# Attention queries: stored in DRAM as high and low parts and read into three slots in turn, instead of split after each load

## The chip, the cores and the metric

The kernel runs on one core of one Trainium2 chip. The metric is device time in microseconds of one execution; the median of several runs counts. Engines are named as in the profile: PE is TensorE (matmuls; PEld its weight loads), DVE is VectorE, ACT is ScalarE, POOL is GpSimd, and SP is SyncE, whose queue issues all the DMAs spoken of here. Each engine takes its instructions strictly in the order of the program and waits on semaphores.

## What is computed

The reference is a two-layer decoder trunk on one sequence of 2048 positions and 1024 features. Layer 0 runs a gated linear recurrence (RG-LRU) and a multi-head latent attention side by side, gates both with SiLU and projects them back; layer 1 is a Mamba-2 SSD mixer; each ends in a residual and a LayerNorm. The change touches only the attention:

```
q = rmsnorm(c_q) @ w_uq                # 8 heads, 64 plain + 32 rotary values each
q_rope = rope(q[..., 64:], cos, sin)
s = (q_nope . k_nope + q_rope . k_rope) * 96 ** -0.5      # causal
p = softmax(s);  y = p @ v
```

The kernel keeps float32 precision out of a matmul type that rounds its operands (float32r): a value x is split into a high part, x rounded to float32r, and a low part, x minus the high part. A product is the sum of three matmuls, high by high, high by low and low by high.

## The kernel before

The program is one instruction list per engine, written out by a Python class. Work is put off with `later(lag, fn)`: the function is called, and so its instructions are written, after `lag` more calls of `tick()`, which stand between the units of matmuls. This order is fixed when the program is built; nothing is reordered at run time.

The stages around the change:

- **Keys and values** (`qkv_begin`, L595): 16 units of keys, each split into one of ten slots of the tile `ring` (128 partitions x 1024, high part in columns 0 to 511, low part in 512 to 1023), then stored to the DRAM tile `d_k`, 512 KB each.
- **Queries** (`phase_qkv`, L641): 32 units, one for each group of a head and a chunk of 512 positions, in the order of `GROUPS` (L35): head pairs 0 to 3, within a pair the chunks 3, 2, 1, 0 (3, 0, 1, 2 for the last pair), within a chunk the two heads. A unit has six matmuls into one of eight PSUM buffers. Its `post` (L660), written one unit later, makes the 128 x 512 float32 tile `qf` (four buffers): DVE multiplies the rotary half by the table (L663), ACT scales and copies the plain half (L664), and SP stores `qf` to `d_q`, 256 KB (L665). In the first eight units the loads of keys into ring slots 0 to 7 (L694, L687) and eight units of values (L602, posts on ACT and DVE) are interleaved.
- **Attention** (`phase_attn`, L708): for each group n, the scores of four rows of 128 queries against all chunks of keys up to the diagonal (three matmuls each, L741 to L743, plus the mask, L745), DVE's maximum of each bank (L746) and the row's minimum of the negated maxima (L750), ACT's exponential with its sum (L762). The transposes of the probabilities (L786), their split (L792 and L129) and the product with the values (L815) of the group before are put between. Group n reads its query from ring slot 8 + n % 2 (L729). Groups of chunk 0 are short (four score banks), those of chunk 3 long (16).

How a query comes back: `load_q(n)` (L698) has SP load `d_q` into a staging tile `st`, one of two buffers shared with the loads of weights. `split_q(n)` (L703) has POOL make the high part (L705) and subtract for the low part (L129, the line of the helper `lo`). In group n the split of group n + 1 is written after the second score bank (L853) and the load of group n + 2 after the third (L855). Group 0's load and split and group 1's load are written inside the query stage (L679 to L682).

SP's queue in the attention also holds, for each group, the load of the next pair's keys (L687, which waits for PE), the store of the softmax sums' reciprocals to `d_li` (L775), the loads of these and of the gate (L811, L812), and the store of the finished output (L834).

Of the kernel before, what the change touches and what calls it, by code (L numbers as in the profile page):

```python
# [7 lines left out]
F32 = mybir.dt.float32  # L8
F32R = mybir.dt.float32r
I32 = mybir.dt.int32  # L10
AF = mybir.ActivationFunctionType
ALU = mybir.AluOpType
AX = mybir.AxisListType

P = 128
# [3 lines left out]
NCH = SEQ // CH  # L19
# [38 lines left out]
class K:  # L58
# [96 lines left out]
    def run(self):  # L155
        nc, tc, A = self.nc, self.tc, self.A
        with ExitStack() as ctx:
            dp = ctx.enter_context(tc.tile_pool(name="dram", bufs=1, space=bass.MemoryType.DRAM))
            core = ctx.enter_context(tc.tile_pool(name="core", bufs=1))
            ctx.enter_context(tc.manual_schedule())  # L160
            self.W = core.tile([P, 10, 2048], F32R, name="W")
            self.core = core
            self.stp = ctx.enter_context(tc.tile_pool(name="stp", bufs=2))
            self.ring = core.tile([P, 10, 1024], F32R, name="ring")
            self.cst = core.tile([P, NCST], F32, name="cst")
            self.im = core.tile([P, 2, 128], F32R, name="im")
            self.half = core.tile([P, 2], F32, name="half")
            nc.vector.memset(self.half[:, 0:1], -0.5)
            nc.vector.memset(self.half[:, 1:2], 0.5)
            self.ident = self.cst[:, C_ID:C_ID + 128]  # L170
            D = self.D = {}
            D["y0"] = dp.tile([NT, P, KB, P], F32, name="d_y0")
            D["sg"] = dp.tile([4, P, SEQ], F32, name="d_sg")
            D["kr"] = dp.tile([NCH, P, 2, 512], F32R, name="d_kr")
            D["q"] = dp.tile([8, NCH, P, 512], F32, name="d_q")
            D["k"] = dp.tile([4, NCH, P, 2, 512], F32R, name="d_k")
            D["x1"] = dp.tile([SEQ, DM], F32, name="d_x1")
            D["x1T"] = dp.tile([NCH, P, KB, 2, 512], F32R, name="d_x1T")
            D["li"] = dp.tile([len(GROUPS), 512], F32, name="d_li")
            D["cs"] = dp.tile([NT, 32, P], F32, name="d_cs")  # L180
            D["tab"] = dp.tile([NCH, 4, P, 4, 5, 8], F32, name="d_tab")
            D["y1"] = dp.tile([NT, P, 16, P], F32, name="d_y1")
            self.pp = ctx.enter_context(tc.tile_pool(name="ps", bufs=8, space=bass.MemoryType.PSUM))
            self.layer0()
            with ExitStack() as c2:
                self.l1c = c2.enter_context(tc.tile_pool(name="l1c", bufs=1))
                self.xst = self.l1c.tile([P, 2, 512], F32, name="xst")
                self.o0 = ExitStack()
                self.phase_out0(self.o0.enter_context(tc.tile_pool(name="o0", bufs=2)))
                with ExitStack() as c3:  # L190
                    self.phase_ssd(c3)
                    self.flush_of("phase_ssd")
            self.phase_out1()
            self.dump()
# [444 lines left out]
        self.vunit = vunit  # L639

    def phase_qkv(self):  # L641
        nc, p = self.nc, self.a3
        cT, D = self.cT, self.D
        T = {}

        def factors(c):

            pt = self.psum()
            for t in range(4):
                nc.tensor.transpose(pt[0:64, t * 128:t * 128 + 128], self.rope[:, 4 * c + t], self.ident)  # L650
            t = T[c] = p.tile([P, 512], F32, tag=f"T{c}", name=f"T{c}", bufs=1)
            for e in range(2):
                nc.scalar.activation(out=t[64 * e:64 * e + 64], in_=pt[0:64], func=AF.Copy, scale=SCALE)

        def qunit(h, c):
            ps = self.psum()
            w = lambda s, kb: self.W[:, 8 + kb, s * 1024 + h * 128:s * 1024 + h * 128 + 128]
            self.mm3(ps, [((w(0, kb), w(1, kb)), (cT[c][:, 0, kb], cT[c][:, 1, kb])) for kb in range(2)])

            def post():  # L660
                qf = p.tile([P, 512], F32, tag="qf", name="qf", bufs=4)
                r, o = (slice(64, 128), slice(0, 64))[::1 - 2 * (h % 2)]
                nc.vector.tensor_tensor(out=qf[r], in0=ps[r], in1=T[c][r], op=ALU.mult)  # L663
                nc.scalar.activation(out=qf[o], in_=ps[o], func=AF.Copy, scale=SCALE)  # L664
                nc.sync.dma_start(out=D["q"][h, c], in_=qf)  # L665
            self.later(2, post)

        for c in (3, 0, 2, 1):
            factors(c)
        self.qst = {}  # L670
        for n, (pr, c, e) in enumerate(GROUPS):
            if n < 8:
                self.attn_kv(n)
            qunit(2 * pr + e, c)
            self.tick()
            if n < 16 - 4 * VB:
                self.vunit(4 * VB + n)
                self.tick()
            if n in (12, 20):  # L679
                self.load_q(n // 20)  # L680
            if n == 16:
                self.split_q(0)  # L682


    def load_k(self, pr, kc, e):
# [4 lines left out]
    def attn_kv(self, i):  # L690
# [4 lines left out]
                               in_=self.D["kr"][kc, r].bitcast(F32).rearrange("p s n -> p (s n)"))  # L695
        self.load_k(0, kc, e)

    def load_q(self, n):  # L698
        pr, c, e = GROUPS[n]
        self.qst[n] = self.stp.tile([P, 512], F32, tag="st", name="st")  # L700
        self.nc.sync.dma_start(out=self.qst[n], in_=self.D["q"][2 * pr + e, c])

    def split_q(self, n):  # L703
        nc, st, t = self.nc, self.qst.pop(n), self.ring[:, 8 + n % 2, :]
        nc.gpsimd.tensor_scalar(out=t[:, 0:512], in0=st, scalar1=1.0, scalar2=0.0, op0=ALU.mult, op1=ALU.add)  # L705
        self.lo(nc.gpsimd, t[:, 512:1024], st, t[:, 0:512])

    def phase_attn(self):  # L708
        nc, A, p, v = self.nc, self.A, self.at, self.nc.vector
        vv = self.W[:, 0:8, :].rearrange("p h (k n) -> p h k n", n=128)  # L710
        ring, D = self.ring, self.D
        N = len(GROUPS)

        im = self.im
        ptx = p.tile([P, 2, 1024], F32R, name="ptx")

        g, li, y = (p.tile([P, 512], F32, name=k) for k in ("g", "li", "y"))
        half = lambda e: slice(64 * e, 64 * e + 64)
# [7 lines left out]
        def scores(n, i):  # L726

            pr, c, e = GROUPS[n]
            q = ring[:, 8 + n % 2, :]  # L729
            qh, ql = q[:, i * 128:i * 128 + 128], q[:, 512 + i * 128:512 + i * 128 + 128]  # L730
            m, banks = mx[(4 * n + i) % 6], {}
            nm = m[:, 4:5] if c else m[:, 0:1]
# [45 lines left out]
        def trans():  # L778

            n, kb = ready.pop(0)  # L780
            pr, c, e = GROUPS[n]
            i0 = max(0, kb - 4 * c)
            ps = self.psum()
            for i in range(i0, 4):
                o = 512 * c * i + 64 * i * (i + 1) + kb * 128
                nc.tensor.transpose(ps[:, i * 128:i * 128 + 128], prob[n][:, o:o + 128], self.ident)  # L786
            self.cnt += 1
            k = self.cnt % 6
            hl = self.W[:, 8 + k // 2, k % 2 * 1024:k % 2 * 1024 + 1024] if k < 4 else ptx[:, k - 4]
            hl = hl.rearrange("p (s n) -> p s n", s=2)  # L790
            w = slice(128 * i0, 512)
            self.later(TL, lambda: nc.scalar.copy(hl[:, 0, w], ps[:, w]))  # L792
            self.later(TL + 1, lambda: self.lo(v, hl[:, 1, w], ps[:, w], hl[:, 0, w]))
            flow.append((n, kb, hl, w))
            if kb == 4 * c + 3:
                prob[n] = None
            if len(flow) > LAG:
                pv()
            self.tick()
# [47 lines left out]
        for n in range(N):  # L847
            pr, c, e = GROUPS[n]
            su = [b for i in range(4) for b in scores(n, i)]
            for i, s in enumerate(su):  # L850
                s()
                self.tick()
                if i == 1 and n + 1 < N:  # L853
                    self.split_q(n + 1)
                if i == 2 and n + 2 < N:  # L855
                    self.load_q(n + 2)
                for _ in range(-(-len(ready) // (len(su) - i + SLACK))):
                    trans()
            if pr < 3:
                self.load_k(pr + 1, c, e)  # L860
            k = n - (N - 9)
            if 0 <= k < 6:
                self.load_at(0, k, A["wo0"][k], 7, (nc.gpsimd, nc.gpsimd))
# [739 lines left out]
```

## Time and profile before

| what | us |
|---|---|
| median of 3 runs | 2680.57 (2680.3 to 2682.99) |
| the profiled execution's own time | 2678.24 |
| its span, first to last instruction | 2676.4 |
| query stage | about 410 to 462 |
| attention | about 462 to 930 |
| POOL's 32 splits, each | 0.62 (L705) + 1.29 (L129) |
| mean granted TensorE clock | 0.994 |

The profile is of one execution. Busy time is summed by engine; a group of instructions has its line, engine, operation and tiles. Idle time just before an instruction is put down to whatever released it: `[2.58 <-POOL ring L705]` means that the engine stood still for 2.58 us until a POOL instruction of line 705, which writes the tile ring, was done. In the list of waits the numbers are the total, how often, and the longest. A row of a table of stretches has the stretch, its length, the busy time of PE, PEld, DVE, ACT and POOL with the number of instructions, the granted TensorE clock as a share of full speed, the busy share of the DMA engines and their GB/s. In rows ordered by time the first two numbers are start and length. "To landing" is the time from the issue of a DMA to its completion.

### The profile page before, as it was taken

To read this page: it belongs to the slowest core of one execution; us is meant where nothing else is said; L and a number is where in the kernel's file an instruction comes from. 1 tells how busy PE (TensorE), PEld (TensorE's weight loads), DVE (VectorE), ACT (ScalarE), POOL (GpSimd) and SP (SyncE) were. 2 spreads that over 40 slices of the span, in tenths; PEclk is the share of its full clock that TensorE was granted. 3 is DMA by queue.
4 is the path that set the end of the run, shared out by engine and by line. 5 is a ranking of instruction groups with operands and counts; after the bars stand their busy time and mean duration, and the time that the engine had idled before them with its cause. 6 is when DMAs were issued, how large, how long until landed. Compare 5 with 4: busy or idle time off the path is not lost.

```text
span 2676.4 us, 40050 instructions
## 1 busy us (share of the span) xinstructions
PE 2610.1 (98%) x14504; PEld 2153.2 (80%) x14504; DVE 1749.6 (65%) x3245; ACT 1531.1 (57%) x3178; POOL 944.2 (35%) x880
## 2 busy tenths in 40 slices
PE   8999999999999999999999999999999999899998
PEld 6888987878787878788888888888888888778886
DVE  7767236878787867875667666666677567745532
ACT  5665335877777732234677766766677667642100
POOL 4446211132324544550334223432343222434421
PEclk9999999999999999999999999999999999999999
DMA  4223328241424456682334333433343333455421
GB/s 140 59 87 118 113 90 284 44 72 43 72 53 85 74 174 196 214 266 95 112 132 159 112 112 108 164 114 112 128 157 123 107 105 118 154 184 210 173 95 40
DMA packets 173111, 334.23 MB, mean 125 GB/s; under 512 B 31985, under 2 KB 90225, under 8 KB 169457
## 3 DMA queue, kind: packets, MB, share of 16 engines
q1 hardware_dynamic: 172912, 331.66, 39.8%
q8 instruction: 115, 1.88, 0.3%
q14 instruction: 84, 0.68, 0.1%
HBM read 245.82 MB, written 85.79 MB: 124 GB/s over the span
## 4 chain that ended last, share of the span: by engine, by line
PE 73%; DVE 10%; ACT 6%; DMA 5%; issue 3%; POOL 1%; SPq 0%; ACTq 0%; POOLq 0%; DVEq 0%
PE ps L1159 9%; PE ps L1161 9%; PE ps L1160 9%; PE ps L137 5%; PE ps L139 4%; PE ps L138 4%; PE ps L786 4%; PE ps L815 4%; PE ps L1409 3%; PE ps L1408 3%; PE ps L1407 3%; PE ps L1262 2%; PE ps L921 2%; PE ps L923 2%; PE ps L922 2%
## 5 line engine op out<-in xcount | busy, mean ns | idle before, releaser
L1159 PE MATMUL ps<-ring,W 128*128 128x512 f32 x768 | 304.6, 397 | 0.0
L1161 PE MATMUL ps<-ring,W 128*128 128x512 f32 x768 | 300.1, 391 | 0.0
L1160 PE MATMUL ps<-ring,W 128*128 128x512 f32 x768 | 299.2, 390 | 0.0
L746 DVE TENSOR_REDUCE mx<-ps 128x1 f32<-128x512 f32 (+3 forms) x320 | 193.5, 608 | 73.9 <-PE ps L743 48.7
L1281 POOL TENSOR_TENSOR y<-y,xs 128x512 f32<-128x512 f32 x60 | 78.8, 1313 | 427.6 <-DVE y L1280 427.6
L762 ACT ACTIVATE pr<-ps,mx 128x512 f32<-128x512 f32 (+3 forms) x320 | 198.5, 629 | 15.8 <-DVE mx L750 11.0
L1159 PE MATMUL ps<-W,ring 128*128 128x512 f32 x512 | 201.3, 393 | 0.0
L1161 PE MATMUL ps<-W,ring 128*128 128x512 f32 x512 | 200.3, 391 | 0.0
L1160 PE MATMUL ps<-W,ring 128*128 128x512 f32 x512 | 199.9, 390 | 0.0
L786 PE MATMUL ps<-cst,pr 128*128 128x128 f32 x1088 | 176.6, 277 | 8.1 <-ACT pr L762 5.9
L1212 ACT ACTIVATE e<-e,tab 128x128 f32<-128x128 f32 x512 | 156.4, 390 | 41.8 <-DMA e<-d_cs 41.8
L1161 PEld LDWEIGHTS ps<-ring,W 128*128 128x128 f32 x768 | 144.1, 188 | 31.2
L1159 PEld LDWEIGHTS ps<-ring,W 128*128 128x128 f32 x768 | 144.3, 188 | 29.7 <-ACT yo L1313 0.9
L1160 PEld LDWEIGHTS ps<-ring,W 128*128 128x128 f32 x768 | 144.4, 188 | 28.9
L129 DVE TENSOR_TENSOR W<-ps,W 128x512 fp32r<-128x512 f32 (+3 forms) x261 | 145.0, 561 | 30.8 <-ACT W L613 18.8
L786 PEld LDWEIGHTS ps<-cst,pr 128*128 128x128 f32 x1088 | 130.6, 142 | 42.0 <-ACT pr L762 11.0
L1127 ACT ACT_TABLE_LOAD x58 | 74.4, 1283 | 149.0 <-DVE xT L1125 79.2
L1392 ACT CAST ring<-ring 128x1024 fp32r<-128x1024 f32 x50 | 50.3, 1045 | 188.7 <-PE ps L1408 99.3
L129 POOL TENSOR_TENSOR ring<-ring 128x1024 fp32r<-128x1024 f32 (+1 forms) x41 | 84.5, 2062 | 189.0 <-ACT ring L1392 160.1
L792 ACT CAST W<-ps 128x512 fp32r<-128x512 f32 (+2 forms) x213 | 110.8, 526 | 67.0 <-PE ps L786 63.0
L129 POOL TENSOR_TENSOR W<-st,W 128x512 fp32r<-128x512 f32 (+2 forms) x70 | 111.4, 1598 | 105.0 <-ACT W L112 90.2
L1125 DVE SCALAR_TENSOR_TENSOR xT<-ps,vec,xT 128x509 f32<-128x509 f32 (+2 forms) x192 | 143.2, 746 | 5.0
(347 smaller groups left out, 7509.7 us busy)
## 6 DMA issues: line engine op xcount, KB each, us to landing
ring<-d_x1T SPq DMA_DIRECT2D x128, 512.0 KB, 7.4
e<-d_cs SPq DMA_DIRECT2D x64, 512.0 KB, 4.4
ring<-d_y SPq DMA_DIRECT2D x25, 1024.0 KB, 4.8
st<-in_w_dram SPq DMA_DIRECT2D x40, 512.0 KB, 5.7
d_x1T<-xt SPq DMA_DIRECT2D x32, 512.0 KB, 4.0
d_y<-yo SPq DMA_DIRECT2D x64, 256.0 KB, 4.9
st<-in_wo_dram SPq DMA_DIRECT2D x24, 512.0 KB, 3.8
xs<-in_xT_dram SPq DMA_DIRECT2D x23, 512.0 KB, 3.9
```

The costliest lines, as they stand in the source:

```text
L129: eng.tensor_tensor(out=out, in0=src, in1=hi.bitcast(F32), op=ALU.subtract)
L137: self.nc.tensor.matmul(ps, ah, bh, start=(i == 0), stop=False)
L138: self.nc.tensor.matmul(ps, ah, bl, start=False, stop=False)
L746: v.tensor_reduce(out=m[:, kc:kc + 1], in_=ps[:, 0:nw], axis=AX.X, op=ALU.max, negate=True)
L762: nc.scalar.activation(out=prob[n][:, o:o + nw], in_=ps[:, 0:nw], func=AF.Exp, bias=nm, accum_out=acc)
L786: nc.tensor.transpose(ps[:, i * 128:i * 128 + 128], prob[n][:, o:o + 128], self.ident)
L792: self.later(TL, lambda: nc.scalar.copy(hl[:, 0, w], ps[:, w]))
L1125: v.scalar_tensor_tensor(out=dst, in0=src, scalar=w(k), in1=dst, op0=ALU.mult, op1=ALU.add)
L1159: nc.tensor.matmul(ps, ah, bh, start=(k == 0), stop=False)
L1160: nc.tensor.matmul(ps, ah, bl, start=False, stop=False)
L1161: nc.tensor.matmul(ps, al, bh, start=False, stop=(k == KB - 1))
L1212: nc.scalar.activation(out=e[:, hd], in_=e[:, hd], func=AF.Relu, scale=-1.0, bias=cs[:, hd:hd + 1])
```

## The change

The queries are split where they are made. `d_q` holds both parts (512 KB for each group). In the query stage the store moves out of `post` into a function `split(qf)`, written one tick after it: the high part is copied into a ring slot (ACT for even n, DVE for odd n; L670 in the new program), POOL subtracts the low part, and SP stores the slot to `d_q` (L672). The slot is 8 + n % 2 for n below 26, and 9 from there on.

In the attention there is no split. `load_q(n)` (L707) reads both parts straight into a slot: ring slot 8, the new tile `q2`, or ring slot 9, in turn (n % 3). Group 0's load is written in the query stage after unit 30, those of groups 1 and 2 at the start of the attention, and that of group n + 2 after the first score bank of group n.

```diff
-            D["q"] = dp.tile([8, NCH, P, 512], F32, name="d_q")
+            D["q"] = dp.tile([8, NCH, P, 2, 512], F32R, name="d_q")
...
-        def qunit(h, c):
+        def qunit(n, h, c):
...
                 nc.scalar.activation(out=qf[o], in_=ps[o], func=AF.Copy, scale=SCALE)
-                nc.sync.dma_start(out=D["q"][h, c], in_=qf)
+                self.later(1, lambda: split(qf))
+
+            def split(qf):
+
+                hl = self.ring[:, 8 + n % 2 if n < 26 else 9].rearrange("p (s n) -> p s n", s=2)
+                (v.tensor_copy if n % 2 else nc.scalar.copy)(hl[:, 0], qf)
+                self.lo(nc.gpsimd, hl[:, 1], qf, hl[:, 0])
+                nc.sync.dma_start(out=D["q"][h, c].bitcast(F32), in_=hl.bitcast(F32))
             self.later(2, post)
...
-            if n in (12, 20):
-                self.load_q(n // 20)
-            if n == 16:
-                self.split_q(0)
+            if n == 30:
+                self.load_q(0)
...
+    def qslot(self, n):
+        return (self.ring[:, 8], self.q2, self.ring[:, 9])[n % 3] if n else self.ring[:, 8]
+
     def load_q(self, n):
         pr, c, e = GROUPS[n]
-        self.qst[n] = self.stp.tile([P, 512], F32, tag="st", name="st")
-        self.nc.sync.dma_start(out=self.qst[n], in_=self.D["q"][2 * pr + e, c])
-
-    def split_q(self, n):
-        nc, st, t = self.nc, self.qst.pop(n), self.ring[:, 8 + n % 2, :]
-        nc.gpsimd.tensor_scalar(out=t[:, 0:512], in0=st, scalar1=1.0, scalar2=0.0, op0=ALU.mult, op1=ALU.add)
-        self.lo(nc.gpsimd, t[:, 512:1024], st, t[:, 0:512])
+        self.nc.sync.dma_start(out=self.qslot(n).bitcast(F32), in_=self.D["q"][2 * pr + e, c].bitcast(F32).rearrange("p s n -> p (s n)"))
...
+        self.q2 = p.tile([P, 1024], F32R, name="q2")
+        for n in (1, 2):
+            self.load_q(n)
...
-            q = ring[:, 8 + n % 2, :]
+            q = self.qslot(n)
...
-                if i == 1 and n + 1 < N:
-                    self.split_q(n + 1)
-                if i == 2 and n + 2 < N:
+                if i == 0 and 0 < n < N - 2:
                     self.load_q(n + 2)
```

More of the change, by code (lines that the diff above doesn't have):

```diff
@@ L641, in phase_qkv @@
     def phase_qkv(self):
-        nc, p = self.nc, self.a3
+        nc, p, v = self.nc, self.a3, self.nc.vector
         cT, D = self.cT, self.D
@@ L669, in phase_qkv @@
             factors(c)
-        self.qst = {}
         for n, (pr, c, e) in enumerate(GROUPS):
@@ L673, in phase_qkv @@
                 self.attn_kv(n)
-            qunit(2 * pr + e, c)
+            qunit(n, 2 * pr + e, c)
             self.tick()
```

## The prediction

> **What bounds the kernel now.** I read the page's first part, then the table of stretches around the edited code, then the waits of TensorE in the attention, then the engines' rows in order of time where the two stages meet.
>
> ```profile
> span 2676.4 us, 40050 instructions
> PE 2610.1 (98%) x14504; PEld 2153.2 (80%) x14504; DVE 1749.6 (65%) x3245; ACT 1531.1 (57%) x3178; POOL 944.2 (35%) x880
> 410.00:465.00 55.00, 54.62 (x235) 42.82 (x235) 32.20 (x55) 29.05 (x57) 3.82 (x4) 1.00 0.91 305
> ```
>
> TensorE is busy 98% of the span, so a change pays only where TensorE waits, and costs wherever it makes it wait. The third row is the stage that makes the queries (columns: stretch, its length, then PE, PEld, DVE, ACT, POOL busy, granted clock, DMA share, GB/s): TensorE is full, POOL nearly unused, DMA 0.91 busy. The attention follows, to about 930 us; TensorE's waits in it, longest in total first:
>
> ```profile
> PE ps L741 <- POOL ring L705: 6.5, 3, 2.6
> PE ps L786 <- ACT pr L762: 4.7, 8, 0.8
> PE ps L743 <- POOL ring L129: 3.0, 4, 0.9
> ```
>
> Waits for POOL's split are 6.5 + 3.0 = 9.5 us, in three places and a trace of a fourth. Where they stand the granted clock drops as well (column after POOL):
>
> ```profile
> 560.00:580.00 20.00, 16.51 (x107) 14.51 (x107) 13.45 (x33) 12.77 (x37) 7.52 (x7) 0.96 0.58 85
> 580.00:600.00 20.00, 19.11 (x95) 14.96 (x94) 15.98 (x37) 14.38 (x42) 7.66 (x7) 0.95 0.43 83
> 700.00:720.00 20.00, 17.88 (x85) 14.40 (x86) 14.97 (x36) 12.19 (x36) 9.32 (x9) 0.91 0.37 84
> 820.00:840.00 20.00, 16.19 (x76) 13.08 (x75) 11.81 (x26) 8.79 (x25) 8.54 (x8) 0.83 0.54 93
> ```
>
> **What goes from the attention.** TensorE's busy time at the missing clock is 16.51 x 0.04 + 19.11 x 0.05 + 17.88 x 0.09 + 16.19 x 0.17 = 6.0 us; these stretches are slow because the wait let the clock fall. With the wait gone, both go: 9.5 + 6.0 = 15.5 us. The lower bound is 9.5 (the clock falls for another reason). Of POOL's 32 splits the rest lay beside other work and is worth nothing.
>
> What is late next? The first such place is group 8, and the load was late because of its place in SP's queue:
>
> ```profile
> 558.26 0.45 SPq L687 DMA_DIRECT2D ring<-d_k  x1
> 564.95 0.59 SPq L701 DMA_DIRECT2D st<-d_q  x1
> 576.25 0.62 POOL L705 TENSOR_SCALAR ring<-st 128x512 fp32r<-128x512 f32 x1 [9.60 <-DMA st<-d_q]
> 576.93 0.33 PE L741 MATMUL ps<-ring 128*128 128x128 f32 x1 [2.58 <-POOL ring L705]
> d_li<-ls SPq DMA_DIRECT2D x28, 2.0 KB, 12.0
> ```
>
> SP's queue from the end of group 5, before (d_li is the 2 KB store of the softmax sums, st the staging tile):
>
> ```order
> L687 DMA ring_66<-d_k_76 64x1024 [waits PE_49]
> L811 DMA li_3751<-d_li_79 64x512 [waits DMAHW7_49,DMAHW2_49]
> L812 DMA g_3750<-d_sg_73 64x512 [waits DMAHW3_49]
> L775 DMA d_li_79<-ls1_3760 128x4x1 [waits DMAHW4_49,DVE_49]
> L834 DMA d_y0_72<-y_3752 64x4x128 [waits DMAHW5_49,Pool_49]
> L701 DMA st_4932<-d_q_75 128x512 [waits DMAHW6_49]
> ```
>
> and after, the same stretch:
>
> ```order
> L691 DMA ring_66<-d_k_76 64x1024 [waits DMAHW1_49,PE_49]
> L707 DMA ring_66<-d_q_75 128x1024 [waits PE_49]
> L815 DMA li_3813<-d_li_79 64x512 [waits DMAHW3_49,DMAHW0_49]
> L816 DMA g_3812<-d_sg_73 64x512 [waits DMAHW4_49]
> L779 DMA d_li_79<-ls1_3822 128x4x1 [waits DMAHW5_49,DVE_49]
> L838 DMA d_y0_72<-y_3814 64x4x128 [waits DMAHW6_49,Pool_49]
> ```
>
> The load of group 8 moves ahead of the slow d_li store: about 559 instead of 564.95 us on this clock. Even with the 11 us that it takes now (564.95 to 576.2) it lands near 570, and TensorE asks at 576.93 - 2.58 = 574.35. So I count the gain whole. The loads double to 512 KB, at a DMA share of 0.37 to 0.58: nothing.
>
> **What comes into the query stage.** Each of 32 units now copies its high part into a slot (ACT for even units, DVE for odd), subtracts on POOL, and stores 512 KB; the slot is free for the next unit only when that store has landed. Slots 8 and 9 alternate up to unit 25; units 26 to 31 all use slot 9. The links, from the same forms elsewhere in the trace (the copies, the subtraction, its hand-over from ACT, the stores):
>
> ```profile
> L221 ACT CAST ring<-xs x29: 606/618/645, 36.0 to 332.9; 128x512 fp32r<-128x512 f32 x29
> L221 DVE CAST ring<-xs x3: 413/415/416, 67.4 to 165.1; 128x512 fp32r<-128x512 f32 x3
> L129 POOL TENSOR_TENSOR ring<-st,ring x32: 1261/1286/1297, 447.4 to 916.2; 128x512 fp32r<-128x512 f32 x32
> 399.24 1.06 ACT L586 CAST W<-st 128x1024 fp32r<-128x1024 f32 x1
> 400.38 2.40 POOL L129 TENSOR_TENSOR W<-st,W 128x1024 fp32r<-128x1024 f32 x1 [12.00 <-ACT W L586]
> L626 SPq DMA_DIRECT2D d_k<-ring x16: 319/326/1352, 387.4 to 414.4; - x16
> DMA to landing us min/median/max: 2.6/3.7/5.3
> d_q<-qf SPq DMA_DIRECT2D x32, 256.0 KB, 2.1
> ```
>
> d_k's store is the nearest row for the new one: 512 KB from a ring slot to a DRAM tile of the same form. Its median of 3.7 us has several stores in flight; here one or two are, so I take the 2.6. A hand-over is 0.08 us (399.24 + 1.06 to 400.38), three per cycle 0.2. One cycle of a slot: 0.62 + 1.29 + 2.6 + 0.2 = 4.7 us with the copy on ACT, 4.5 on DVE. Bounds: 2.1 us landing (the 256 KB row) and 3.7. Two slots give a unit every 2.35 us, one slot every 4.6. TensorE makes a unit in 6 matmuls, and starts one 0.7 us after three:
>
> ```profile
> 437.77 0.47 PE L137 MATMUL ps<-cT,W 128*128 128x512 f32 x1
> 438.54 0.40 PE L137 MATMUL ps<-cT,W 128*128 128x512 f32 x1
> 439.24 0.39 PE L137 MATMUL ps<-cT,W 128*128 128x512 f32 x1
> 411.53 0.69 DVE L663 TENSOR_TENSOR qf<-ps,T 64x512 f32<-64x512 f32 x1
> 437.65 2.19 DVE L663 TENSOR_TENSOR qf<-ps,T 64x512 f32<-64x512 f32 x3
> 461.89 0.68 DVE L663 TENSOR_TENSOR qf<-ps,T 64x512 f32<-64x512 f32 x1 [0.63 <-ACT qf L664]
> 462.50 0.27 DVE L746 TENSOR_REDUCE mx<-ps 128x1 f32<-128x128 f32 x1
> 462.97 2.05 DVE L746 TENSOR_REDUCE mx<-ps 128x1 f32<-128x512 f32 x3 [0.19 <-PE ps L743]
> 465.05 0.16 DVE L750 TENSOR_REDUCE mx<-mx 128x1 f32<-128x4 f32 x1
> 465.32 1.28 ACT L762 ACT_TABLE_LOAD   x1 [2.11 <-DMA d_q<-qf]
> ```
>
> So 1.4 us a unit now (three starts from 437.77 to 439.24): the slots become slower than TensorE. The wait stands on ACT and DVE, and both run in order. DVE at the end of the stage, before (the products of the last two units, then the first row's maxima):
>
> ```order
> L663 TENSOR_TENSOR qf_3736<-ps_3718,T2_3295 64x512 [waits DMAHW0_49,PE_49,Activation_49]
> L663 TENSOR_TENSOR qf_3740<-ps_3729,T2_3295 64x512 [waits DMAHW1_49,PE_49,Activation_49]
> L746 TENSOR_REDUCE mx0_3753<-ps_3766 128x1 [waits PE_49]
> L746 TENSOR_REDUCE mx0_3753<-ps_3772 128x1 [waits PE_49]
> L746 TENSOR_REDUCE mx0_3753<-ps_3779 128x1 [waits PE_49]
> ```
>
> and after, where L670 is the copy into the slot and DMAHW the landing of the store ahead:
>
> ```order
> L670 CAST ring_66<-qf_3748 128x512 [waits DMAHW5_49,DMAHW6_49,DVE_49,Pool_49]
> L663 TENSOR_TENSOR qf_3774<-ps_3754,T1_3303 64x512 [waits PE_49]
> L663 TENSOR_TENSOR qf_3788<-ps_3767,T2_3295 64x512 [waits PE_49]
> L670 CAST ring_66<-qf_3774 128x512 [waits DMAHW0_49,DMAHW7_49,DVE_49,Pool_49]
> L663 TENSOR_TENSOR qf_3794<-ps_3781,T2_3295 64x512 [waits PE_49]
> L670 CAST ring_66<-qf_3794 128x512 [waits DMAHW2_49,DMAHW3_49,DVE_49,Pool_49]
> L750 TENSOR_REDUCE mx0_3815<-ps_3828 128x1 [waits PE_49]
> ```
>
> The attention's maxima, and behind them ACT's exponentials, are queued behind the copy of unit 31. When does that run? Units 0 to 8 are paced by DVE and ACT already (411.53 to 437.65); one more copy per unit, (0.62 + 0.42) / 2 = 0.5 us, puts unit 8's product near 441.7, and its copy, behind two activations, at 443. From 8 to 24 eight cycles: 443 + 8 x 4.7 = 480.6. Unit 25's subtraction follows unit 24's on POOL and ends at 480.6 + 0.7 + 2 x 1.29 = 483.9; its store lands 486.5; copies 26 to 31 are five cycles apart from first to last, 3 x 4.7 + 2 x 4.5 = 23.1, so copy 31 starts at 486.6 + 23.1 = 509.7 and ends at 510.1. Four maxima and the minimum (0.27 + 2.05 + 0.16, some 0.2 between) end at 512.8, where ACT loads its table; now that is at 465.32. Delay: 47.5 us. Fourteen landings lie in the chain: 2.1 us would make it 40.5, 3.7 us 63; unit 8's start is good to about 3 us. POOL's part (32 x 1.29 us) is in the cycle; that two-input work with DVE at its side could slow it is inside these bounds.
>
> **Sum.** 2678.24 (the profiled execution: span 2676.4 and 1.84 around it) + 47.5 - 15.5 = 2710.2. The median of the runs shown, 2680.57, is 2.3 higher, so I forecast 2712 us, 1.2% slower. What a measurement here can tell from no change is about 0.2%, 5 us.
>
> **The rivals.**
>
> *Faster: the slots never bind.* Store and subtraction hide behind TensorE, and only the gain is left: 2680.6 - 15.5 = 2665. It decides if a slot's cycle is under two units of TensorE, 2.8 us. For it: POOL is idle there, and the old store had four buffers and hardly stalled. Against: 1.29 + 2.1 alone are 3.4. Chance 0.07; that gain and delay cancel, 0.02.
>
> *Stores land at the median.* 3.7 us, since DMA is 0.91 busy in this stage: 47.5 becomes 63, 2728. Against: the waiting thins the stores out. The Trainium skill (DMA: Bandwidth & Descriptors, Bandwidth) lists 0.95 us for 64 KB and 6.15 us for 1 MB, which I interpolate to an estimate of 3.4 us for 512 KB; by that the sum would be about 2723. Those were loads on another issue path; the row here says 2.6 at its quickest. Chance 0.18.
>
> *The loads stay late.* The change doesn't do what it is said to do in the attention: d_li stores still sit before the loads, TensorE waits as now: 2712 + 15.5 = 2727. Against: the queue above. Chance 0.12.
>
> *TensorE works ahead.* While the copies wait it fills all eight PSUM buffers with scores, 8 x 0.7 = 5.6 us done in the shade: 2707. Against: now too it meets full buffers at once in group 0, paced by ACT:
>
> ```profile
> 467.12 0.44 PE L741 MATMUL ps<-ring 128*128 128x384 f32 x1 [0.29 <-ACT pr L762]
> ```
>
> Chance 0.06. My forecast: 0.55.
>
> **Range.** Its low end is the quick store, 2712 - 7 = 2705, less 5.6 for working ahead and 2 for unit 8: 2697. Its high end is the slow store with the loads nearly all late, 2728 + 10 = 2738. Slower takes all but the first rival and its neighbour: 0.91; same 0.02; faster 0.07.
>
> **What would show it.** The ACT table load of the attention's first exponential near 513 us; copies L670 whose idle time ends on the landing of d_q's store, about 2 to 3 us each; POOL's subtractions 2.35 us apart in the stage's middle and 4.6 us at its end; TensorE with a hole of tens of us before 513; no wait of L741 or L743 for POOL or for the load of q, and a clock of 1.00 in the four stretches, moved by the delay. If the stage ends before 480 us, or TensorE waits for ring at the starts of groups 8, 16 and 24, a step is wrong.

## The result, and the profile after

| | us |
|---|---|
| changed kernel, median of 4 runs | 2718.5 (2715.94 to 2720.53) |
| kernel before, on the same chip, median of 4 | 2681.78 (2680.3 to 2683.98) |
| ratio | 1.0136, 95% interval 1.0118 to 1.0153 |
| the profiled execution after, its own time and span | 2720.29, 2718.5 |

The change costs 36.7 us. The forecast was 2712 us, 31 us (1.2%) over the median shown then.

The first rows of the page, and the rows of the lines that are new (of a copy: durations in ns as least/median/most, first and last start in us; below them what ended their idle time, with total and count; then how long d_q's stores, L672, take to land):

```profile
span 2718.5 us, 40043 instructions
PE 2614.4 (96%) x14504; PEld 2153.2 (79%) x14504; DVE 1757.5 (65%) x3261; ACT 1541.3 (57%) x3194; POOL 922.6 (34%) x848
L670 ACT CAST ring<-qf x16: 617/620/622, 418.1 to 512.9; 128x512 fp32r<-128x512 f32 x16
L670 DVE CAST ring<-qf x16: 418/427/1032, 421.5 to 517.6; 128x512 fp32r<-128x512 f32 x16
  DMA d_q<-ring: 67.4, 26
DMA to landing us min/median/max: 2.6/2.6/4.7
```

TensorE does the same work (2614.4 us busy, 2610.1 before) in a span 42.1 us longer. ACT and DVE stand still for 67.4 us before the copies into the slots, 26 times, until a store of d_q has landed (one more wait, of 2.9 us, is put down to ACT). The slots bind. The landing row rests on few stores: the trace tells the landing of three of the 32.

ACT in order of time, even units only (start, duration, idle before and its releaser): unit 8, the three after it, unit 24, the last units 26, 28 and 30, and the table load of the first exponential:

```profile
447.71 0.62 ACT L670 CAST ring<-qf 128x512 fp32r<-128x512 f32 x1
452.43 0.62 ACT L670 CAST ring<-qf 128x512 fp32r<-128x512 f32 x1 [0.94 <-DMA d_q<-ring]
457.13 0.62 ACT L670 CAST ring<-qf 128x512 fp32r<-128x512 f32 x1 [0.97 <-DMA d_q<-ring]
461.83 0.62 ACT L670 CAST ring<-qf 128x512 fp32r<-128x512 f32 x1 [1.04 <-DMA d_q<-ring]
...
487.09 0.62 ACT L670 CAST ring<-qf 128x512 fp32r<-128x512 f32 x1 [0.20 <-DMA d_q<-ring]
494.17 0.62 ACT L670 CAST ring<-qf 128x512 fp32r<-128x512 f32 x1 [2.75 <-DMA d_q<-ring]
503.36 0.62 ACT L670 CAST ring<-qf 128x512 fp32r<-128x512 f32 x1 [2.73 <-DMA d_q<-ring]
512.86 0.62 ACT L670 CAST ring<-qf 128x512 fp32r<-128x512 f32 x1 [2.72 <-DMA d_q<-ring]
520.30 1.28 ACT L766 ACT_TABLE_LOAD   x1 [6.82 <-DVE mx L754]
```

The cycle of a slot is read from row to row: 4.7 us three times running, and 9.2 to 9.5 us for two units where one slot is left. The table load comes 55.0 us later than before (465.32).

Unit 31's copy on DVE, SP's load of the first group and its time to landing, TensorE's first score, the semaphore waits of that line on TensorE's sequencer (in ns, the longest is 27284), the waits of the queries' matmuls (410 to 530 us), and the granted clock where TensorE waits (column after POOL):

```profile
517.59 0.43 DVE L670 CAST ring<-qf 128x512 fp32r<-128x512 f32 x1 [8.08 <-DMA d_q<-ring]
505.77 0.37 SPq L707 DMA_DIRECT2D ring<-d_q  x1
DMA to landing us min/median/max: 3.9/3.9/3.9
509.87 0.45 PE L745 MATMUL ps<-ring 128*128 128x128 f32 x1 [25.79 <-DVE qf L663]
L745 PEldq EVENT_SEMAPHORE  x165: 51/51/27284, 482.4 to 976.2; - x165
PE ps L137 <- ACT qf L664: 15.8, 17, 2.8
480.00:500.00 20.00, 1.67 (x6) 1.04 (x6) 6.51 (x11) 5.40 (x9) 8.22 (x7) 0.71 0.42 172
500.00:520.00 20.00, 7.96 (x26) 6.38 (x26) 4.22 (x9) 3.01 (x5) 5.71 (x5) 0.61 0.34 131
```

Up to 482 us TensorE waits 17 times, 15.8 us in all, for ACT to empty a buffer. It has made unit 31 by 484.08. Then it stands still for 25.79 us, and this wait is of another kind: ACT has emptied the buffer that the first score needs (unit 24's) by 483.62, and what is missing is the query of group 0. Its load is written after unit 30, so it stands in SP's queue behind unit 30's late store, is issued at 505.77 and lands at 509.67. The row of the first score names DVE's product of unit 31 (done at 509.51) instead, but the sequencer's wait from 482.4, 27.28 us long, ends with the landing. This wait doesn't set the table load: the eight banks that TensorE can fill are done by 517.83, before DVE has ended unit 31's copy (518.02) and can begin the maxima.

In the attention the waits for the split are gone. TensorE's longest waits there, 540 to 985 us, and its clock in three stretches that stand about where the slow ones of before stood, moved by the delay:

```profile
PE ps L790 <- ACT pr L766: 5.0, 8, 1.1
PE ps L819 <- ACT pr L766: 2.2, 3, 0.7
PE ps L790 <- DVE W L129: 1.1, 3, 0.4
620.00:640.00 20.00, 19.23 (x123) 16.45 (x122) 15.95 (x38) 14.31 (x40) 2.55 (x2) 1.00 0.70 102
740.00:760.00 20.00, 19.27 (x123) 16.81 (x122) 16.57 (x37) 13.56 (x38) 2.55 (x2) 1.00 0.75 73
860.00:880.00 20.00, 19.28 (x122) 16.61 (x120) 16.65 (x38) 13.78 (x39) 2.56 (x2) 1.00 0.68 100
```

No wait for POOL or for a load of q is left among them, and the clock is full. The attention ends where the first matmul of the next stage's line begins (L921 before, L923 now: first and last start behind the durations):

```profile
L921 PE MATMUL ps<-W,ring x256: 388/389/498, 957.3 to 1167.9; 128*128 128x512 f32 x128
```

```profile
L923 PE MATMUL ps<-W,ring x256: 388/389/498, 998.0 to 1208.5; 128*128 128x512 f32 x128
```

So the attention runs to 957.3 us in the trace of before, not to the 930 of the table further up. With these three marks (unit 0's product on DVE, the table load, this first matmul) the time splits in two: before 411.53, 465.32, 957.3; now 413.30, 520.30, 998.0. The table load is 55.0 us later, of which 1.8 is there before unit 0 is done; from the table load to the end of the attention it takes 477.7 us instead of 492.0, 14.3 less. The rest of the program keeps the 40.7 us and adds 1.4.

### The profile page after: what moved, and what is told of

It reads as the page before. It is cut to its first block, busy times and chain, and to the rows that moved or that the text cites. A ratio compares the mean times of both kernels' runs of the same rounds, so it can differ in the third digit from the quotient of the medians.

```text
span 2718.5 us, 40043 instructions
## 1 busy us (share of the span) xinstructions
PE 2614.4 (96%) x14504; PEld 2153.2 (79%) x14504; DVE 1757.5 (65%) x3261; ACT 1541.3 (57%) x3194; POOL 922.6 (34%) x848
## 4 chain that ended last, share of the span: by engine, by line
PE 74%; DVE 10%; ACT 6%; DMA 5%; issue 3%; POOL 2%; SPq 0%; ACTq 0%; DVEq 0%; POOLq 0%
PE ps L1161 9%; PE ps L1163 9%; PE ps L1162 9%; PE ps L137 5%; PE ps L139 4%; PE ps L138 4%; PE ps L819 4%; PE ps L790 4%; PE ps L1410 4%; PE ps L1409 4%; PE ps L1411 4%; DMA d_q<-ring 2%; PE ps L1264 2%; PE ps L923 2%; PE ps L925 2%
## 5 line engine op out<-in xcount | busy, mean ns | idle before, releaser
L1129 ACT ACT_TABLE_LOAD x58 | 74.4, 1283 | 148.7 <-DVE xT L1127 79.2
```

## The experiments

Theory: in the query stage the slots' cycle (copy, subtraction, landing) sets the pace, and the delay passes whole to the end; in the attention the gain comes from the load's place ahead of d_li's store in SP's queue. Rivals: the stage is bound by POOL or by the bytes, whatever the slots; and the gain comes from taking the split off POOL.

The runs came on four chips, each beside before: 2681.51 us (median of 13) for the first four, 2696.58 (14) for the next three, 2697.52 (15) for the four after, 2697.02 (17) for the last. Kernels are compared with before of their own row, and with each other on one chip only.

| kernel | median us | ratio to before, 95% | unit 0's product | table load | attention ends |
|---|---|---|---|---|---|
| four slots | 2684.84 | 1.0016 (1.0006 to 1.0025) | 411.71 | 486.00 | 962.5 |
| one slot | 2773.16 | 1.0343 (1.0327 to 1.0358) | 413.91 | 574.21 | 1052.5 |
| before, early load | 2668.2 | 0.9954 (0.9939 to 0.9969) | 412.32 | 466.23 | 945.1 |
| after, late load | 2729.45 | 1.0174 (1.0157 to 1.0191) | 413.96 | 520.47 | 1013.2 |
| two slots to the end | 2711.22 | 1.0054 (1.0033 to 1.0074) | 412.98 | 507.52 | 990.3 |
| two stores | 2707.81 | 1.0036 (1.0022 to 1.005) | 414.67 | 504.39 | 986.7 |
| four slots, DVE helps | 2695.11 | 0.9997 (0.9986 to 1.0008) | 413.01 | 490.02 | 978.5 |
| changed kernel again | 2727.12 | 1.0106 (1.0091 to 1.0121) | 412.68 | 518.80 | 1004.5 |
| two slots again | 2712.42 | 1.0048 (1.0031 to 1.0064) | 413.15 | 507.37 | 994.5 |
| two stores again | 2706.39 | 1.0035 (1.0022 to 1.0048) | 411.13 | 499.45 | 985.4 |
| both | 2701.48 | 1.0019 (1.0004 to 1.0034) | 414.85 | 500.10 | 985.1 |
| both, first load earlier | 2700.44 | 1.0013 (1.0002 to 1.0025) | 416.78 | 498.11 | 981.9 |

**Four slots.** The two ring slots and two staging buffers of the same size take turns (from unit 28 on, ring slot 9 and the staging buffers).

```diff
+    def hslot(self, n):
+        k = n % 4 if n < 28 else (1, 2, 2)[(n - 28) % 3]
+        if k < 2:
+            return self.ring[:, 8 + k].rearrange("p (s n) -> p s n", s=2)
+        return self.stp.tile([P, 2, 512], F32R, tag="st", name="st")
-                hl = self.ring[:, 8 + n % 2 if n < 26 else 9].rearrange("p (s n) -> p s n", s=2)
+                hl = self.hslot(n)
```

> The changed kernel, but the query stage splits into four slots in turn instead of two and then one: ring slots 8 and 9 and the two staging buffers that the queries no longer use. Slot theory: what delays the stage is the wait of the copy for the landing of an earlier store; four slots at 4.7 us a cycle give a unit every 1.2 us, less than TensorE's 1.4, so nearly the whole delay of 53 us goes and the attention's gain of 14 us is left: 2670 to 2682 us, ACT's first exponential table load near 470 us. Rate theory (twice the bytes, or POOL's 32 subtractions, set the stage whatever the slots): 2710 to 2718 us.

Measured: 3.3 us over before and 2.8 over the slots' range; the table load at 486.00, 20.7 us later than before and 34.3 earlier than in the changed kernel. Its rows in the stage, the stores' landings (median us, from 410 to 490, of the six and the one whose landing the trace tells), the load of group 0 and TensorE's wait:

```profile
430.00:450.00 20.00, 19.22 (x78) 13.63 (x77) 12.59 (x22) 10.44 (x20) 10.53 (x9) 1.00 0.97 350
450.00:470.00 20.00, 14.88 (x62) 11.08 (x60) 13.64 (x20) 11.77 (x20) 16.63 (x14) 1.00 0.82 333
d_q<-ring SPq DMA_DIRECT2D x16, 512.0 KB, 3.4
d_q<-st SPq DMA_DIRECT2D x16, 512.0 KB, 7.5
476.00 0.38 SPq L713 DMA_DIRECT2D ring<-d_q  x1
PE ps L751 <- DVE ring L676: 15.0, 1, 15.0
```

So 34.3 of the 55.0 us of delay are the slots. With them gone the transfers (DMA 0.97 busy) and then POOL (16.63 of 20 us) are the busiest; which of them sets the pace is not shown. TensorE still waits 15.0 us: the row names DVE's last copy (ended 479.51), but group 0's load, issued at 476.00 behind the stores, lands at 480.23, and the first score starts at 480.43. That remainder was in neither theory as a cost of its own.

**One slot.** Units 0 to 25 as well go through slot 9.

```diff
-                hl = self.ring[:, 8 + n % 2 if n < 26 else 9].rearrange("p (s n) -> p s n", s=2)
+                hl = self.ring[:, 9].rearrange("p (s n) -> p s n", s=2)
```

> The changed kernel, but all 32 units use slot 9. Slot theory: a unit every 4.6 us from the start, so some 17 x 2.3 = 39 us more in units 8 to 25 and 10 to 20 us more in the first eight: 2765 to 2780 us. Rate theory: the bytes and the work are the same, 2718 us.

Measured 2773.16 us, as the slots' theory has it. Even units on ACT:

```profile
538.81 0.62 ACT L670 CAST ring<-qf 128x512 fp32r<-128x512 f32 x1 [2.76 <-DMA d_q<-ring]
548.02 0.62 ACT L670 CAST ring<-qf 128x512 fp32r<-128x512 f32 x1 [2.73 <-DMA d_q<-ring]
```

9.2 us for two units (548.02 less 538.81), 4.6 for one. The table load is 108.9 us later than before, the attention 13.7 us shorter: 95.2, against a measured difference of 91.7.

**Before with an early load.** The split stays on POOL; only the load of group n + 2 moves from behind the third score bank to behind the first (not for the last groups).

```diff
-                if i == 2 and n + 2 < N:
+                if i == (0 if n < N - 9 else 2) and n + 2 < N:
                     self.load_q(n + 2)
```

> The kernel before, with one edit: the load of group n + 2 is written after the first score bank of group n instead of the third (up to group 22; later groups as before, because the staging buffers are shared with weights there). The split on POOL stays. Theory of the queue: TensorE's waits at groups 8, 16 and 24 come from the load's place behind the slow d_li store, so they and the low clock behind them go: 2666 to 2671 us. Rival: they come from POOL's split, which only the removal ends: 2678 to 2682 us.

Measured 2668.2 us, 13.3 less than before, and the fastest kernel of this study on its chip. Of TensorE's waits for POOL, 9.5 us in before, one of 0.4 is left; POOL does its 32 splits as ever:

```profile
PE ps L743 <- POOL ring L129: 0.4, 1, 0.4
```

The attention takes 478.9 us, against 477.7 in the changed kernel. Nearly the whole gain of the change there, 13.1 of 14.3 us, can be had by moving one load; taking the split off POOL is worth 1.2 us at most by these two traces.

**After with a late load.** The counterpart: the changed kernel with its loads behind the third bank.

```diff
-                if i == 0 and 0 < n < N - 2:
+                if i == 2 and 0 < n < N - 2:
                     self.load_q(n + 2)
```

> The changed kernel with one edit: the load of group n + 2 is written after the third score bank of group n, as in the kernel before, behind the d_li store. Theory of the queue: the load lands about 2 us after TensorE asks at groups 8, 16 and 24, so 6 to 12 of the 14 us come back: 2724 to 2731 us, and TensorE's waits at L745 are put down to the load of q. Rival (the split was the cause): 2717 to 2720 us, no such waits.

Measured 2729.45 us, 47.9 over before, where the changed kernel is 36.7 over: 11.2 us of the gain are lost, as the queue's theory has it. The profiled execution, 2736.91 us, is the slowest of the four, so its stages are on the long side: its attention takes 492.7 us, as long as before's 492.0 though nothing is split in it. TensorE waits for transfers (from 540 to 985 us; below, one such wait, then the issue of a load of q, the longest wait, and SP's wait for that load, from 855 to 890 us), and the loads of q take long (median us to landing of those few that the trace tells, 540 to 940 us):

```profile
PE ps L745 <- DMA q<-d_q: 1.7, 1, 1.7
866.86 0.55 SPq L707 DMA_DIRECT2D ring<-d_q  x1
882.82 0.45 PE L745 MATMUL ps<-ring 128*128 128x128 f32 x1 [7.51 <-DMA li<-d_li]
SPq L98 <- DMA ring<-d_q: 4.6, 1, 4.6
ring<-d_q SPq DMA_DIRECT2D x17, 512.0 KB, 12.3
q<-d_q SPq DMA_DIRECT2D x9, 512.0 KB, 13.5
d_li<-ls SPq DMA_DIRECT2D x26, 2.0 KB, 14.4
```

The wait of 7.51 us is put down to a load of li, which scores don't read. The load of q issued at 866.86 has landed at 882.68, when SP, which waits for it too (L98), goes on; TensorE starts at 882.82. So this wait is one for the load of q as well. The same loads in the changed kernel, issued ahead of d_li's store:

```profile
ring<-d_q SPq DMA_DIRECT2D x18, 512.0 KB, 3.5
q<-d_q SPq DMA_DIRECT2D x9, 512.0 KB, 3.4
```

3.5 against 12 to 13 us: here a load that is issued behind the 2 KB store (14.4 us to landing) lands about when that store does. With the run above, the place in the queue is shown to be the cause of the gain, from both sides. The late place does two things, which these runs don't part: group 8's load is issued 5.5 us later (621.69 against 616.22), and such loads take some 9 us longer to land.

**Two slots to the end.** Units 26, 28 and 30 use a staging buffer, the odd ones slot 9.

```diff
+        if n == 26:
+            self.qt = self.stp.tile([P, 2, 512], F32R, tag="st", name="st")
+        if n >= 26 and n % 2 == 0:
+            return self.qt
+        return self.ring[:, 8 + n % 2].rearrange("p (s n) -> p s n", s=2)
```

> The changed kernel, but units 26 to 31 alternate between slot 9 and one of the free staging buffers, so the stage has two slots to its end. Slot theory: the last six units come 2.35 us apart instead of 4.65, six times 2.3 is 14 us less: 2703 to 2707 us. If the tail's pace were set by the bytes or by POOL, it would stay at 2718 us.

**Two stores.** The high part is stored as soon as it is copied, while POOL makes the low part: two stores of 256 KB.

```diff
                 (v.tensor_copy if n % 2 else nc.scalar.copy)(hl[:, 0], qf)
+                nc.sync.dma_start(out=D["q"][h, c, :, 0].bitcast(F32), in_=hl[:, 0].bitcast(F32))
                 self.lo(nc.gpsimd, hl[:, 1], qf, hl[:, 0])
-                nc.sync.dma_start(out=D["q"][h, c].bitcast(F32), in_=hl.bitcast(F32))
+                nc.sync.dma_start(out=D["q"][h, c, :, 1].bitcast(F32), in_=hl[:, 1].bitcast(F32))
```

> The changed kernel, but each part is stored by a DMA of its own: the high part right behind its copy, the low part behind POOL's subtraction, 256 KB each, the same slots and bytes. Landing theory: the link that frees the slot is now a 256 KB store of 2.1 us instead of a 512 KB one of 2.6, fourteen links are 7 us less: 2709 to 2713 us. If the landing were set by the bytes in flight, nothing changes: 2718 us; if 64 issues instead of 32 crowd SP's queue, 2720 us and more.

**Four slots, DVE helps.** In the kernel with four slots every fourth subtraction goes to DVE.

```diff
-                self.lo(nc.gpsimd, hl[:, 1], qf, hl[:, 0])
+                self.lo(nc.gpsimd if n % 4 else v, hl[:, 1], qf, hl[:, 0])
```

> The kernel with four slots, but DVE instead of POOL subtracts in every fourth unit, which takes POOL from 1.29 to 0.97 us a unit. The table load of the first exponential stood 20.7 us later than before with four slots. If POOL sets that stage's pace (16.6 of 20 us busy in its middle), a good part of it goes: 2674 to 2680 us. If the DMA engines do (share 0.97 to 0.82, 350 to 333 GB/s), it stays: 2683 to 2687 us.

These three ran on a chip where before takes 15 us longer, so their absolute expectations can't be held against them, only ratios and marks. Both shorter cycles helped: the table load came 12.8 and 15.9 us earlier than in the changed kernel's profile. The last is inconclusive: 1.5 us under before (interval 0.9986 to 1.0008), where four slots alone had been 3.3 over on the other chip; its table load, at 490.02, is no earlier than the 486.00 there, and TensorE waits 15.4 us for the first score (15.0 there). That POOL sets the pace with four slots is thus not shown; these marks speak against it.

**All on one chip.** To size the two shorter cycles, the changed kernel ran again beside them, and a kernel with both edits.

> The changed kernel once more, so that the three runs beside it can be measured against it on the same chip. On the first chip it took 36.7 us more than before. If the two chips differ only by a constant (before took 15 us more on the second one), the difference stays 35 to 39 us here; if the slower chip also hides part of the stage's delay, it is under 32 us. First exponential's table load 54 to 56 us later than before's.

> Two slots up to the last unit, as in e5. Theory (the delay is the chain of slot cycles and reaches the end whole): 12 to 14 us less than the changed kernel on the same chip, since the table load came 12.8 us earlier in e5. Rival (the last six units' wait is partly hidden by later work): under 8 us less.

> High and low part stored by themselves, as in e6. Theory: 14 to 17 us less than the changed kernel on the same chip (table load 15.9 us earlier in e6). Rival (64 stores crowd the transfers behind them, so part is lost later): under 11 us less.

> Both edits in one kernel. Theory, the cycles add: unit 8's copy at 448, a cycle of 3.9 us as in e6 (448.1 to 479.2 in eight), three more for the last units, so the table load near 497 us, 23 us before the changed kernel's, and the time 20 to 25 us less than the changed kernel. Rival, with two slots and quick stores the transfers bound the stage: no more than 17 us less.

The changed kernel takes 29.6 us more than before here: not the 35 to 39 of a mere constant between the chips, but the under 32 of the other theory. Its table load is about where it was (518.80, 53.5 us later than in the trace of before from the first chip; 54 to 56 were expected), but its attention takes 485.7 us instead of 477.7. Before was not profiled on this chip, so what its own 16 us are, and what hides part of the delay, stays open. Against the changed kernel on this chip, two slots save 14.7 us, two stores 20.7, both 25.6, each more than its theory's span (by 0.6 to 3.7 us) and far over its rival's, though the four runs with two slots alone spread over 10 us. Each saves at least what its table load gains (11.4, 19.3 and 18.7 in the single profiles): the stage's delay does pass to the end. That the two edits add is not shown: two slots save 14.7 us alone, but only 4.9 on top of two stores, and the table load of both comes 3 us later than the 497 expected.

Two stores gain more than their first expectation counted, which was 7 us for fourteen landings shorter by 0.5 us; the table load moved by 15.9 and 19.3 us. In the profile from this chip, two even units on ACT, two odd ones on DVE, and the store of the first odd one's high part:

```profile
447.66 0.62 ACT L670 CAST ring<-qf 128x512 fp32r<-128x512 f32 x1
451.35 0.62 ACT L670 CAST ring<-qf 128x512 fp32r<-128x512 f32 x1
448.77 1.16 DVE L670 CAST ring<-qf 128x512 fp32r<-128x512 f32 x1 [1.10 <-DMA d_q<-ring]
450.08 0.38 SPq L671 DMA_DIRECT2D d_q<-ring  x1
452.48 1.15 DVE L670 CAST ring<-qf 128x512 fp32r<-128x512 f32 x1 [1.11 <-DMA d_q<-ring]
```

The cycle is 3.7 us instead of 4.7. The copy on DVE waits only for the landing of the high part's store, which is issued right behind the copy before, at 450.08; POOL waits for the low part's by itself (0.53 us before 450.17). So the two halves of a slot come free apart, and the subtraction is no longer a link in the copy's cycle.

With both edits the copies start by 490.67 (unit 30) and 494.76 (unit 31, on DVE), and the table load comes at 500.10. TensorE's longest wait from 410 to 530 us in that kernel shows a second thing that ends there:

```profile
PE ps L753 <- DMA ring<-d_q: 18.3, 1, 18.3
```

As with four slots, TensorE's first score, at 494.05, waits for group 0's load: it is written behind unit 30 and stands in SP's queue behind the stores of units that POOL has yet to finish.

**Both, first load earlier.** The kernel with both edits, and group 0's load two units earlier in the queue.

```diff
-            if n == 30:
+            if n == 28:
                 self.load_q(0)
```

> Both edits, and the load of group 0 written behind unit 28 instead of unit 30, so that it stands four stores (two units) earlier in SP's queue. Theory (with both edits it is this load that releases TensorE): the load is issued near 486 instead of 489.4 us, TensorE's first score comes 3 to 5 us earlier than at 494.05, and from unit 0's product to the table load it takes 80 to 83 us instead of 85.3; the time is within 0.2% of before. Rival (the load waits in the queue for slot 8, holds the last stores up, and unit 31's copy sets the end as before): 85 to 87 us from unit 0's product to the table load, and the time 0.2 to 0.3% over before, as with both edits alone.

Measured 2700.44 us, 3.4 over before; both edits alone were 4.0 over, and the two intervals overlap. The load, TensorE's first score, and DVE's copies of units 29 and 31:

```profile
486.49 0.37 SPq L715 DMA_DIRECT2D ring<-d_q  x1
491.14 0.45 PE L753 MATMUL ps<-ring 128*128 128x128 f32 x1 [13.45 <-DMA d_q<-ring]
491.72 0.43 DVE L677 CAST ring<-qf 128x512 fp32r<-128x512 f32 x1 [3.95 <-DMA d_q<-ring]
494.31 1.52 DVE L677 CAST ring<-qf 128x512 fp32r<-128x512 f32 x1 [1.45 <-ACT st L677]
```

Counted from unit 0's product, since the stage itself began 1.9 us later here, the first score comes after 74.4 us instead of 79.2, and the table load after 81.3 instead of 85.3: the marks moved as the theory has it. Unit 31's copy moved with them less far (77.5 us instead of 79.9), and unit 29's now waits 3.95 us for a landing; the first row's maxima stand behind the last copy on DVE. The row of the first score names a store of d_q; the load itself has landed at 490.89, just before it. So the load and the last copies end close together, and of the 4 us little is seen in the time. No version of the stored split came under before by more than the measurement can tell.

## Why the prediction was right, step by step

- **The slots are slower than TensorE, and DVE's and ACT's order carries the wait into the attention.** Right: 67.4 us of idle copies, DVE's maxima and ACT's table load behind unit 31's copy, and the run with one slot, whose delay grows as the cycle says. TensorE's hole of 25.79 us is there as forecast, but ends otherwise: the load of group 0, which stands behind late stores in SP's queue, has no term in the prediction. Here it lands early enough to cost nothing; with four slots it is what TensorE waits for.
- **The cycle of 4.7 us.** Right to a tenth, with 2.6 us as its landing; of the three stores whose landing the trace tells, the two in the stage's middle took 2.6 us as well. The rival that stores land at 3.7 us is out, since the measured cycle has no room for it; the estimate of 3.4 us drawn from the Trainium skill (DMA: Bandwidth & Descriptors, Bandwidth) is also above what these stores take.
- **The delay of 47.5 us, mis-sized.** It is 55.0, and the 7.5 more come in pieces: 1.8 is there before unit 0; unit 8's copy is a further 2.9 late, since units 0 to 8 wait for landings already (I had them paced by DVE and ACT alone); the eight cycles from unit 8 to 24 take 39.4 us instead of 37.6, six of them 4.7 and two longer; from unit 24 to 26 it takes 7.1 instead of 6.0, since unit 25's subtraction does not follow unit 24's at once but waits for a copy that waits for its own slot; the last five cycles take 23.4 (23.1 forecast), and from copy 31 to the table load 2.7 (3.1 forecast).
- **The gain of 15.5 us.** 14.3 in the trace, by the means forecast: the waits for POOL are gone and the clock is 1.00. Of the step's parts the load's place in the queue was the one that mattered: the early load alone does it, with the split still on POOL.
- **TensorE works ahead**, a rival: worth nothing that shows. Group 0's load lands at 509.67, late in the hole; TensorE does fill eight banks before the maxima begin, yet the attention behind the hole is only 1.2 us shorter than that of before with the early load, which has no such hole.
- **The sum.** 2710.2 for the profiled execution became 2720.29: 7.5 from the delay, 1.2 from the gain, 1.4 behind the attention. The medians differ by 5.3 us less than the two profiled executions do: that of before was under the three runs shown first, that of after among the slower of its four.

## What to carry to other kernels

A buffer that is stored whole, and so holds its value until that store has landed, costs copy, arithmetic and landing together; divide that by the number of buffers, compare it with the producer's time for one value, and follow the wait along the engines that run in order, since what is queued behind it pays. When a wait goes away after several things changed, try the cheapest of them alone: here moving one load ahead of a slow small store in the queue gave nearly the whole gain (2668.2 us, 0.5% under before) and needed no new store.

## What the runs showed of the hardware that was not expected

- DVE's copy of 128 x 512 takes 0.42 us alone and up to 1.03 us in the changed kernel while POOL subtracts; with two stores, where POOL is denser, its median is 0.97 us. In both kernels every copy that takes longer than 0.43 us ends 0.28 to 0.29 us after the subtraction that it overlaps, whenever it began: it ends at 459.39 against 459.10 and at 469.47 against 469.18 in the changed kernel, at 449.93 against 449.65 with two stores. So DVE's copy is held until POOL is done (the prediction had allowed for the reverse, a slower POOL). ACT's copy stays at 0.62 and POOL's subtraction at 1.28. The row of the copies with two stores:

```profile
L670 DVE CAST ring<-qf x16: 417/974/1157, 419.4 to 496.7; 128x512 fp32r<-128x512 f32 x16
```

- A 512 KB store lands in 2.6 us with one or two in flight. With four slots the six whose landing the trace tells took 2.9 to 6.4 us (median 3.4), and one from a staging buffer 7.5 us, issued at 428.0, while keys and values were moved as well; the DMA share was up to 0.97 there. More slots bring less than their number.
- The two longer cycles between units 8 and 24 of the changed kernel fall where a transfer of the instruction queues stands beside the stores, from 464 to 468 us (1.1% of the engines' time) and from 476 to 479 us (3.5%). That these transfers held the stores up is only argued from their place; no run tested it.
